# Up projection of a gated MLP with tokens on the output partitions, and each section's down projection one block later

## The chip, the cores and the metric

The kernel runs on one core of one Trainium2 chip. The metric is device time in microseconds (us), the median of several executions of the same program. Beside it there is one profiled execution, from which every row below is taken; its engines are PE (TensorE), DVE (VectorE), ACT (ScalarE), POOL (GpSimd) and SP (SyncE).

## The reference, cut to what matters

One decoder layer on 256 tokens of width 2048: a forgetting-attention mixer, then a gated MLP. Only the MLP and the step ahead of it change.

```python
h = h + fox_mixer(rms_norm(h, mix_norm), ...)          # q, k, v, attention, w_out
h = h + conv_ffn(rms_norm(h, ffn_norm), ...)

def conv_ffn(h, w_up, conv_w, conv_b, w_down):
    up = h @ w_up                                       # 256 x 2048 @ 2048 x 11264
    padded = jnp.pad(up, ((0, 0), (2, 0), (0, 0)))
    y = conv_b + conv_w[0] * padded[:, 0:seq]           # three causal taps along the tokens
    for tap in range(1, 3):
        y = y + conv_w[tap] * padded[:, tap:tap + seq]
    gate, val = jnp.split(y, 2, axis=-1)                # 5632 each
    return (jax.nn.silu(gate) * val) @ w_down           # 5632 x 2048
```

All of it is float32. The kernel multiplies with float32r operands: it splits every operand in a rounded part (hi) and the rest (lo) and adds three products, hi·hi, hi·lo and lo·hi.

## The kernel before, in words

**Weights.** `split_load` (L157) brings 1 MB (four k-rows of 128 by 512 columns) into one of four `raw` buffers through SP's DMA queue. ACT rounds it into `hi` and DVE subtracts to get `lo`, in two pieces of 128x1024 (two k-rows) each. There are five `hi` and five `lo` buffers (`HBUF`), so at most ten of a product's sixteen k-rows are prepared ahead of PE.

**Order.** The program is written as straight code. Work that is spread behind PE sits in the list `bg`, of which `tick` takes one step after every half of a weight load. The compiler's scheduler then orders each engine's instructions; each engine runs its own list in order.

**Output projection** (`out_part`, `out_evac`). Four column chunks c of 512; tokens are on the output partitions, with `mm_t` (L285): for each of the two token tiles t, three matmuls of 512 columns (L289 to L291), activations stationary and weights moving. `out_evac` adds the chunk to the residual `res`; the MLP wants it turned, channels on the partitions (`hs`). Chunks 0 to 2 are turned by DVE's transposes (32x32 squares in place, L315) and `spread` (L255), 16 DMAs from POOL that carry each 32x32 square to its place; chunk 3 is turned by PE (`h_turn`).

**Up projection** (`up_half`, `mm_run`). 11 blocks b of 512 gate columns ("ug") and 512 value columns ("uv"), a half being one of the two. Channels come out on the partitions: for each of the 16 k-rows and each 128 channels i, one matmul with `hi` stationary and both activation parts moving (512 columns, L278), and one with `lo` stationary and the rounded activations moving (256 columns, L280). `taps` adds the two parts (ACT copy L663, DVE add L664), multiplies by 1/rms of each token (`rhB`, L667, made by four PE matmuls in `spread_rstd`, L643), and does the three taps (ACT L669, DVE L673 twice). Then SiLU on ACT, the product, and the hi/lo split of the result `gt`.

**Down projection** (`down`). The 11 blocks form sections of 3, 3, 3 and 2. After the last block of a section its down projection runs with `mm_t`: four chunks of 512 output columns, over the section's 12 (or 8) k-rows.

Of the kernel before, what the change touches and what calls it, by code (L numbers as in the profile page):

```python
# [24 lines left out]
FT = FF // P  # L25
# [6 lines left out]
SECTIONS = [12, 12, 12, 8]  # L32
# [62 lines left out]
def trunk_kernel(  # L95
# [61 lines left out]
    def split_load(src, kk, n, name):  # L157
        raw = wraw.tile([P, WEL], F32, tag="raw", name=f"raw_{name}")
        nc.sync.dma_start(raw[:, 0 : kk * n], src)
        hv, lv = [], []  # L160
        step = max(1, HEL // n)
        for j in range(0, kk, step):
            w = min(step, kk - j)
            hi = whi.tile([P, HEL], F32R, tag="hi", name=f"hi_{name}_{j}")
            lo = wlo.tile([P, HEL], F32R, tag="lo", name=f"lo_{name}_{j}")
            src = raw[:, j * n : (j + w) * n]
            nc.scalar.copy(hi[:, 0 : w * n], src)  # L167
            nc.vector.tensor_tensor(  # L168
                lo[:, 0 : w * n], src, hi[:, 0 : w * n].bitcast(F32), op=ALU.subtract
            )  # L170
# [101 lines left out]
    hs = []  # L272
    hs_new = lambda: [acts.tile([P, 2, S], F32R, tag=f"as{k}", name=f"hs{k}") for k in range(KT)]


    def mm_run(run):
        for o, hv, lv, a, first, last in run:
            nc.tensor.matmul(o[:, 0:512], lhsT=hv, rhs=a.rearrange("p a s -> p (a s)"), start=first, stop=False)  # L278
        for o, hv, lv, a, first, last in run:
            nc.tensor.matmul(o[:, 0:S], lhsT=lv, rhs=a[:, 0, :], start=False, stop=last)  # L280

    wo = Blocks(w_out, blocks_out())


# [18 lines left out]
    def out_evac(pts, c):  # L303
        for t in range(NT):
            hc = res[:, t, c * 512 : (c + 1) * 512]
            nc.vector.tensor_tensor(hc, hc, pts[t], op=ALU.add)
            sq = hp_.tile([P, 512], F32, tag="hsq", name=f"hsq{c}_{t}")
            square(sq, t, c)
        if c == 3:
            bg.extend([nop, lambda: [h_turn(kp) for kp in (6, 7)]])  # L310
            return
        hq = tp.tile([P, 4 * NT, P], F32, tag="hq", name=f"hq{c}")
        hT = tp.tile([P, NT, 4, P], F32, tag="hT", name=f"hT{c}")
        for t in range(NT):
            nc.vector.transpose(  # L315
                hq[:, 4 * t : 4 * t + 4, :].rearrange("p k s -> p (k s)"), res[:, t, c * 512 : (c + 1) * 512]
            )
        spread(hT.rearrange("p t k s -> p (t k) s"), hq, nc.gpsimd)

        def scale():  # L320
            for j in range(4):
                k = 4 * c + j
                g, d = gffn[:, k : k + 1], hs[k].rearrange("p a (t s) -> p a t s", t=NT)
                nc.scalar.activation(d[:, 0], hT[:, :, j, :], AF.Copy, scale=g)
                nc.vector.scalar_tensor_tensor(
                    d[:, 1], hT[:, :, j, :], g, d[:, 0].bitcast(F32), op0=ALU.mult, op1=ALU.subtract,
                )
# [307 lines left out]
    nc.gpsimd.dma_start(convp.rearrange("p j f -> p (j f)"), conv)  # L635

    rh = const.tile([P, NT], F32, name="rh")
    rhB = const.tile([P, S], F32, name="rhB")

    def spread_rstd():  # L640
        prb = bank("prb")
        for t in range(NT):
            nc.tensor.matmul(  # L643
                prb[:, t * P : (t + 1) * P], lhsT=rh[:, t : t + 1].to_broadcast([P, P]), rhs=ident,
                start=True, stop=True,
            )
        nc.vector.tensor_copy(rhB, prb[:, 0:S])

    rms(rh)
    bg.extend([nop, spread_rstd])  # L650

    NPAD = 6
    pads = [fp.tile([P, S + 2], F32, name=f"pad{j}") for j in range(NPAD)]
    for j in range(NPAD):
        nc.gpsimd.memset(pads[j][:, 0:2], 0.0)
    npad = [0]

    wu = Blocks(w_up, blocks_up())
    wd = Blocks(w_down, blocks_down())

    def taps(pt, f, name):
        t = fp.tile([P, S], F32, tag="ut", name=f"ut{name}", bufs=2)
        nc.scalar.copy(t, pt[:, S:512])  # L663
        nc.vector.tensor_tensor(t, pt[:, 0:S], t, op=ALU.add)  # L664
        pad = pads[npad[0] % NPAD]
        npad[0] += 1
        nc.vector.tensor_tensor(pad[:, 2 : S + 2], t, rhB, op=ALU.mult)  # L667
        y = fp.tile([P, S], F32, tag="y", name=f"y{name}", bufs=4)
        nc.scalar.activation(  # L669
            y, pad[:, 0:S], AF.Identity, bias=convp[:, 3, f : f + 1], scale=convp[:, 0, f : f + 1]  # L670
        )
        for j in (1, 2):
            nc.vector.scalar_tensor_tensor(  # L673
                y, pad[:, j : j + S], convp[:, j, f : f + 1], y, op0=ALU.mult, op1=ALU.add
            )
        return y

    def gtile(b):
        return acts.tile([P, 2, 2, S], F32R, tag=f"os{b % 8}", name=f"gt{b}")

    def up_half(b, half, name):
        pts = [bank(f"p{name}{b}_{i}", ("mm", "sm")[i // 2]) for i in range(4)]
        for kb in range(4):
            hv, lv = split_load(wu[b, half, 4 * kb], 4, 512, f"{name}{b}_{kb}")
            mm_run([
                (pts[i], hv[j][:, i * P : (i + 1) * P], lv[j][:, i * P : (i + 1) * P],
                 hs[k], k == 0, k == KT - 1)
                for j, k in enumerate(range(kb * 4, kb * 4 + 4)) for i in range(4)
            ])
            tick()  # L690
            tick()
        return pts

    def up_block(b):
        sgs = []
        for i, pt in enumerate(up_half(b, 0, "ug")):
            f = 4 * b + i
            yg = taps(pt, f, f"g{f}")
            sg = fp.tile([P, S], F32, tag="sg", name=f"sg{f}", bufs=5)
            nc.scalar.activation(sg, yg, AF.Silu)  # L700
            sgs.append(sg)
        gts = []
        for i, pt in enumerate(up_half(b, 1, "uv")):
            f = 4 * b + i
            if i % 2 == 0:
                gpair = gtile(f // 2)
            yv = taps(pt, FT + f, f"v{f}")
            nc.vector.tensor_tensor(yv, sgs[i], yv, op=ALU.mult)
            gt = gpair[:, i % 2]
            nc.scalar.copy(gt[:, 0, :], yv)  # L710
            nc.vector.tensor_tensor(gt[:, 1, :], yv, gt[:, 0, :].bitcast(F32), op=ALU.subtract)
            gts.append(gt)
        return gts

    outv = out.rearrange("o (t p) d -> p (o t) d", p=P)

    def down(s, f0, gts, last):
        nk = len(gts)
        for c in range(4):
            pts = [bank(f"pd{s}_{c}_{t}", ("mm", "sm")[t]) for t in range(NT)]  # L720
            k0 = 0
            while k0 < nk:
                kk = min(4, nk - k0)
                hv, lv = split_load(wd[c, f0 + k0], kk, 512, f"d{s}_{c}_{k0}")
                for j in range(kk):
                    mm_t(pts, gts[k0 + j], hv[j], lv[j], k0 + j == 0, k0 + j == nk - 1)
                k0 += kk
            for t in range(NT):
                hc = res[:, t, c * 512 : (c + 1) * 512]
                nc.vector.tensor_tensor(hc, hc, pts[t], op=ALU.add)  # L730
                if last:
                    nc.sync.dma_start(outv[:, t, c * 512 : (c + 1) * 512], hc)

    f0 = 0
    for s, n in enumerate(SECTIONS):
        gts = []
        for b in range(n // 4):
            gts += up_block(f0 // 4 + b)
        while bg:
            tick()  # L740
        down(s, f0, gts, s == 3)
        f0 += n


# [47 lines left out]
```

## Time and profile before

| | us |
|---|---|
| device time, median of 3 runs | 1122.23 (1120.85 to 1123.55) |
| device time of the profiled execution | 1121.05 |
| its span, first to last instruction | 1119.3 |
| PE busy in the span | 1110.5 |
| DVE busy | 753.2 |
| ACT busy | 570.5 |
| POOL busy | 87.6 |

The profiled execution is 1.18 us below the median of the runs. "Busy" counts an engine's instructions only, not its waits; a matmul's end is modelled, so times of matmuls are best read from start to start.

### The profile page before, as it was taken

The page shows a single profiled execution, that of the slowest core. Times are in us where ns is not written, and L with a number is a line of the kernel's source. Part 1 is how long each engine was busy: PE and PEld are TensorE (multiplying, and loading weights), DVE is VectorE, ACT ScalarE, POOL GpSimd, SP SyncE. Part 2 cuts the span into 40 slices and gives each one's busy share as a digit, 9 for nine tenths or more (in the row PEclk, how much of TensorE's full clock was granted, in tenths as well). Part 3 has the DMA queues.
Part 4 walks back from the last instruction along what each step waited for, and adds up shares of the span by engine and source line. Part 5 has one row for each costly group of instructions (what it writes and reads, how often), then busy time and mean ns, then how long its engine had stood idle before and what let it go on. Part 6 is the DMA issues. An engine that isn't in the chain of part 4 may idle for free.

```text
span 1119.3 us, 15032 instructions
## 1 busy us (share of the span) xinstructions
PE 1110.5 (99%) x5672; PEld 950.0 (85%) x5672; DVE 753.2 (67%) x1210; ACT 570.5 (51%) x837; POOL 87.6 (8%) x152
## 2 busy tenths in 40 slices
PE   8999999999999999999999999999999999999998
PEld 6898888888888888888888888888888888888886
DVE  6666948677647658687655767765577777557864
ACT  7644545454535656565444555543455554346542
POOL 1102403030106400000000000000000000000000
PEclk9999999999999999999999999999999999999999
DMA  9839577677648645555555555555555555555542
GB/s 336 312 76 357 140 264 224 176 266 209 217 157 239 215 168 188 189 188 190 197 200 171 196 192 192 193 201 188 188 188 188 189 188 193 197 183 183 198 176 75
DMA packets 89145, 223.51 MB, mean 200 GB/s; under 512 B 58624, under 2 KB 58912, under 8 KB 64752
## 3 DMA queue, kind: packets, MB, share of 16 engines
q1 hardware_dynamic: 86640, 218.52, 57.8%
q0 software_dynamic: 2288, 4.01, 1.5%
q8 instruction: 44, 0.72, 0.2%
q14 instruction: 29, 0.24, 0.1%
q10 hardware_dynamic: 144, 0.02, 0.0%
HBM read 212.28 MB, written 2.11 MB: 192 GB/s over the span
## 4 chain that ended last, share of the span: by engine, by line
PE 96%; SPq 1%; DMA 1%; DVE 1%; ACT 0%; issue 0%; DVEq 0%
PE pug L278 14%; PE puv L278 14%; PE puv L280 8%; PE pug L280 7%; PE pd L290 7%; PE pd L289 7%; PE pd L291 7%; PE po L291 3%; PE pk L355 3%; PE pk L354 3%; PE po L290 3%; PE po L289 3%; PE pk L353 3%; PE pq L354 2%; PE pq L355 2%; PE pq L353 2%
## 5 line engine op out<-in xcount | busy, mean ns | idle before, releaser
L278 PE MATMUL puv<-hs,hi_uv 128*128 128x512 f32 x704 | 168.8, 391 | 1.2 <-ACT hi_uv L167 1.1
L278 PE MATMUL pug<-hs,hi_ug 128*128 128x512 f32 x704 | 167.9, 391 | 0.0
L168 DVE TENSOR_TENSOR lo_ug<-raw_ug,hi_ug 128x1024 fp32r<-128x1024 f32 x88 | 106.1, 1221 | 81.1 <-PE puv L280 36.8
L168 DVE TENSOR_TENSOR lo_d<-raw_d,hi_d 128x1024 fp32r<-128x1024 f32 x88 | 106.6, 1223 | 78.6 <-ACT hi_d L167 56.1
L278 PEld LDWEIGHTS puv<-hs,hi_uv 128*128 128x128 f32 x704 | 129.2, 188 | 26.9 <-ACT hi_uv L167 1.6
L278 PEld LDWEIGHTS pug<-hs,hi_ug 128*128 128x128 f32 x704 | 129.6, 188 | 25.2
L167 ACT CAST hi_d<-raw_d 128x1024 fp32r<-128x1024 f32 x88 | 92.2, 1052 | 114.8 <-PE pd L291 83.0
L167 ACT CAST hi_uv<-raw_uv 128x1024 fp32r<-128x1024 f32 x88 | 92.4, 1051 | 106.7 <-PE pug L278 63.2
L167 ACT CAST hi_ug<-raw_ug 128x1024 fp32r<-128x1024 f32 x88 | 92.6, 1052 | 105.9 <-PE puv L278 34.4
L168 DVE TENSOR_TENSOR lo_uv<-raw_uv,hi_uv 128x1024 fp32r<-128x1024 f32 x88 | 106.2, 1221 | 58.5 <-PE pug L280 47.2
L290 PE MATMUL pd<-lo_d,gt 128*128 128x512 f32 x352 | 136.2, 389 | 0.0
L289 PE MATMUL pd<-hi_d,gt 128*128 128x512 f32 x352 | 134.5, 389 | 0.0
L291 PE MATMUL pd<-hi_d,gt 128*128 128x512 f32 x352 | 134.2, 389 | 0.0
L280 PEld LDWEIGHTS puv<-hs,lo_uv 128*128 128x128 f32 x704 | 90.3, 191 | 3.4
L280 PEld LDWEIGHTS pug<-hs,lo_ug 128*128 128x128 f32 x704 | 90.3, 191 | 3.4
L280 PE MATMUL puv<-hs,lo_uv 128*128 128x256 f32 x704 | 91.5, 283 | 0.0
L280 PE MATMUL pug<-hs,lo_ug 128*128 128x256 f32 x704 | 91.3, 283 | 0.0
L291 PEld LDWEIGHTS pd<-hi_d,gt 128*128 128x128 f32 x352 | 66.1, 188 | 13.7
L289 PEld LDWEIGHTS pd<-hi_d,gt 128*128 128x128 f32 x352 | 66.1, 188 | 13.6
L290 PEld LDWEIGHTS pd<-lo_d,gt 128*128 128x128 f32 x352 | 66.1, 188 | 13.6
L168 DVE TENSOR_TENSOR lo_o<-raw_o,hi_o 128x1024 fp32r<-128x1024 f32 x32 | 39.1, 1222 | 34.2 <-ACT hi_o L167 33.8
L168 DVE TENSOR_TENSOR lo_q<-raw_q,hi_q 128x1024 fp32r<-128x1024 f32 (+1 forms) x33 | 38.8, 1187 | 27.0 <-ACT hi_q L167 27.0
(171 smaller groups left out, 1816.7 us busy)
## 6 DMA issues: line engine op xcount, KB each, us to landing
raw_ug<-in_w_up SPq DMA_DIRECT2D x44, 1024.0 KB, 4.9
raw_uv<-in_w_up SPq DMA_DIRECT2D x44, 1024.0 KB, 4.9
raw_d<-in_w_down SPq DMA_DIRECT2D x44, 1024.0 KB, 4.8
raw_k<-in_w_in SPq DMA_DIRECT2D x16, 1024.0 KB, 8.8
raw_o<-in_w_out SPq DMA_DIRECT2D x16, 1024.0 KB, 5.6
raw_q<-in_w_in SPq DMA_DIRECT2D x12, 1024.0 KB, 6.0
raw_v<-in_w_in SPq DMA_DIRECT2D x12, 1024.0 KB, 5.7
raw_q<-in_w_in SPq DMA_DIRECT2D x7, 512.0 KB, 6.8
```

What stands on the lines that cost most here:

```text
L167: nc.scalar.copy(hi[:, 0 : w * n], src)
L168: nc.vector.tensor_tensor(lo[:, 0 : w * n], src, hi[:, 0 : w * n].bitcast(F32), op=ALU.subtract)
L278: nc.tensor.matmul(o[:, 0:512], lhsT=hv, rhs=a.rearrange("p a s -> p (a s)"), start=first, stop=False)
L280: nc.tensor.matmul(o[:, 0:S], lhsT=lv, rhs=a[:, 0, :], start=False, stop=last)
L289: nc.tensor.matmul(pts[t], lhsT=ah, rhs=hv, start=first, stop=False)
L290: nc.tensor.matmul(pts[t], lhsT=ah, rhs=lv, start=False, stop=False)
L291: nc.tensor.matmul(pts[t], lhsT=al, rhs=hv, start=False, stop=last)
L353: nc.tensor.matmul(o, lhsT=ah, rhs=hv[j], start=(k == 0), stop=False)
L354: nc.tensor.matmul(o, lhsT=ah, rhs=lv[j], start=False, stop=False)
L355: nc.tensor.matmul(o, lhsT=al, rhs=hv[j], start=False, stop=(k == KT - 1))
```

## The change

The up projection takes the form of the output projection: tokens on the output partitions, `hs` stationary, weights moving, three matmuls of 512 columns a token tile (`mm_t`), two PSUM banks a half where there were four. 1/rms of a token is now a per-partition scale of the evacuation (ACT), so `rhB`, its matmuls and the multiply go. The half is then turned: two DVE transposes of 128x512, and `spread` from POOL. `taps` reads the turned tile, without a pad. The taps of a half (`gates`, `values`) are written behind the matmuls of the next half or of the next weight load in `down`. Down projections of sections 0 and 1 are written behind the first block of the next section. Chunk 2 of the output projection is turned by PE like chunk 3.

```diff
-        if c == 3:
-            bg.extend([nop, lambda: [h_turn(kp) for kp in (6, 7)]])
+        if c >= 2:
+            bg.extend([nop, lambda: [h_turn(kp) for kp in (2 * c, 2 * c + 1)]])
             return
...
     def up_half(b, half, name):
-        pts = [bank(f"p{name}{b}_{i}", ("mm", "sm")[i // 2]) for i in range(4)]
+        pts = [bank(f"p{name}{b}_{t}", "mm") for t in range(NT)]
         for kb in range(4):
             hv, lv = split_load(wu[b, half, 4 * kb], 4, 512, f"{name}{b}_{kb}")
-            mm_run([
...
+            for j in range(4):
+                k = 4 * kb + j
+                mm_t(pts, hs[k], hv[j], lv[j], k == 0, k == KT - 1)
             tick()
             tick()
+        uq = tp.tile([P, 4, NT, P], F32, tag="hq", name=f"q{name}{b}")
+        uT = tp.tile([P, 4, S], F32, tag="hT", name=f"T{name}{b}")
+        for t in range(NT):
+            nc.scalar.activation(
+                uq[:, :, t, :], pts[t].rearrange("p (f d) -> p f d", d=P), AF.Copy, scale=rh[:, t : t + 1]
+            )
+        for f in range(0, 4, 2):
+            q = uq[:, f : f + 2].rearrange("p f t d -> p (f t d)")
+            nc.vector.transpose(q, q)
+        spread(
+            uT.rearrange("p f (t s) -> p (f t) s", t=NT), uq.rearrange("p f t d -> p (f t) d"), nc.gpsimd
+        )
+        return uT
...
+    def taps(u, f, name):
+        y = fp.tile([P, S], F32, tag="y", name=f"y{name}", bufs=4)
+        nc.scalar.activation(y, u, AF.Identity, bias=convp[:, 3, f : f + 1], scale=convp[:, 2, f : f + 1])
+        for j in (1, 0):
+            d = 2 - j
+            nc.vector.scalar_tensor_tensor(
+                y[:, d:S], u[:, 0 : S - d], convp[:, j, f : f + 1], y[:, d:S], op0=ALU.mult, op1=ALU.add
+            )
+        return y
...
+    def up_block(b):
+        for half, name, use in ((0, "ug", gates), (1, "uv", values)):
+            uT = up_half(b, half, name)
+            product_done()
+            later.append(lambda uT=uT, use=use: use(b, uT))
...
+                if k0 == 0:
+                    product_done()
...
+    behind = [ends[0] + 1, ends[1] + 1, FT // 4, FT // 4]
+    done = 0
     for s, n in enumerate(SECTIONS):
-        gts = []
-        for b in range(n // 4):
-            gts += up_block(f0 // 4 + b)
...
+        while done < behind[s]:
+            up_block(done)
+            done += 1
+        down(s, starts[s], n, s == len(SECTIONS) - 1)
```

How this changes the engines' lists is shown at three places, all in the second block or at its edge. Numbers behind a name are buffer numbers; a name's own indices stand before them (`hi_ug_1_0` is weight load 1, k-row 0 of that load).

PE, the start of the second block's gate half, before: of a weight load's 32 rows, the first of 512 and the first of 256 columns.

```order
L278 MATMUL pug_0_4009<-hs_2726,hi_ug_0_0_4015 128x512
L278 MATMUL pug_1_4010<-hs_2726,hi_ug_0_0_4015 128x512
L278 MATMUL pug_2_4011<-hs_2726,hi_ug_0_0_4015 128x512
L278 MATMUL pug_3_4012<-hs_2726,hi_ug_0_0_4015 128x512
L278 MATMUL pug_0_4009<-hs_2727,hi_ug_0_0_4015 128x512
...
L278 MATMUL pug_3_4012<-hs_2729,hi_ug_0_2_4019 128x512
L280 MATMUL pug_0_4009<-hs_2726,lo_ug_0_0_4016 128x256
```

The same place in the changed kernel: of a weight load's 24 rows, those of the first k-row.

```order
L282 MATMUL pug_0_3896<-hi_ug_0_0_3900,hs_2726 128x512
L283 MATMUL pug_0_3896<-lo_ug_0_0_3901,hs_2726 128x512
L284 MATMUL pug_0_3896<-hi_ug_0_0_3900,hs_2726 128x512
L282 MATMUL pug_1_3897<-hi_ug_0_0_3900,hs_2726 128x512
L283 MATMUL pug_1_3897<-lo_ug_0_0_3901,hs_2726 128x512
L284 MATMUL pug_1_3897<-hi_ug_0_0_3900,hs_2726 128x512
```

Per half PE issues 96 matmuls of 512 columns where it issued 64 of 512 and 64 of 256; the lo weights are wanted one matmul after the hi weights, where they were wanted 16 matmuls after.

ACT, behind the second block's gate half, before: PSUM copies (`utg`), taps (`yg`), SiLU (`sg`) and rounding of weights (`hi`) alternate.

```order
L663 COPY utg_4181<-pug_0_4009 128x256
L663 COPY utg_4191<-pug_1_4010 128x256
L167 CAST hi_uv_2_2_4315<-raw_uv_2_4309 128x1024
L669 ACTIVATE yg_4185<-pad_3547,convp 128x256
L663 COPY utg_4201<-pug_2_4011 128x256
L669 ACTIVATE yg_4195<-pad_3548,convp 128x256
L663 COPY utg_4211<-pug_3_4012 128x256
L167 CAST hi_uv_3_0_4353<-raw_uv_3_4351 128x1024
```

ACT in the changed kernel, where the second block's value half (`puv`) ends and the third block's gate half is being prepared; `Tug` is the second block's turned gate half.

```order
L167 CAST hi_ug_1_2_4312<-raw_ug_1_4306 128x1024
L649 ACTIVATE quv_4224<-puv_0_4086,rh 128x4x128
L662 ACTIVATE yg_4246<-Tug_4035,convp 128x256
L662 ACTIVATE yg_4252<-Tug_4035,convp 128x256
L662 ACTIVATE yg_4258<-Tug_4035,convp 128x256
L662 ACTIVATE yg_4264<-Tug_4035,convp 128x256
L649 ACTIVATE quv_4224<-puv_1_4087,rh 128x4x128
L167 CAST hi_ug_2_0_4342<-raw_ug_2_4340 128x1024
```

The taps of a gate half now stand one half later, between the two evacuations of the value half, and the rounding of the next half's fifth weight piece (`hi_ug_2_0`) stands behind all of them.

DVE at that same edge in the changed kernel.

```order
L168 TENSOR_TENSOR lo_ug_1_2_4313<-raw_ug_1_4306,hi_ug_1_2_4312 128x1024
L665 SCALAR_TENSOR_TENSOR yg_4246<-Tug_4035,convp,yg_4246 128x255
L665 SCALAR_TENSOR_TENSOR yg_4252<-Tug_4035,convp,yg_4252 128x255
...
L665 SCALAR_TENSOR_TENSOR yg_4258<-Tug_4035,convp,yg_4258 128x254
L654 STREAM_TRANSPOSE quv_4224<-quv_4224 128x512 x2
L665 SCALAR_TENSOR_TENSOR yg_4264<-Tug_4035,convp,yg_4264 128x254
L168 TENSOR_TENSOR lo_ug_2_0_4343<-raw_ug_2_4340,hi_ug_2_0_4342 128x1024
```

Seven of the gate half's eight taps, the two transposes of the value half and the eighth tap stand ahead of `lo_ug_2_0`, which before was made ahead of any of them.

## Rows read from the trace of the kernel before

**Rows 1.** The page's first lines and its chain that ended last.

```profile
span 1119.3 us, 15032 instructions
PE 1110.5 (99%) x5672; PEld 950.0 (85%) x5672; DVE 753.2 (67%) x1210; ACT 570.5 (51%) x837; POOL 87.6 (8%) x152
PE 96%; SPq 1%; DMA 1%; DVE 1%; ACT 0%; issue 0%; DVEq 0%
```

**Rows 2.** The chain in order of time, section 1: start us, us, what.

```profile
584.90 3.63 PE pug L278 x16
588.52 1.91 PE pug L280 x16
590.44 3.65 PE pug L278 x16
...
716.56 1.91 PE puv L280 x16
718.47 0.23 PE pd L289
...
783.78 3.63 PE pug L278 x16
```

**Rows 3.** Windows: us, busy of PE, PEld, DVE, ACT, POOL, clock, DMA share, GB/s.

```profile
584.90:718.47 133.57, 133.57 (x769) 118.06 (x769) 91.73 (x146) 73.49 (x111) 0.00 (x0) 1.00 0.55 189
718.47:783.78 65.31, 65.31 (x289) 54.08 (x289) 41.94 (x56) 28.25 (x35) 0.00 (x0) 1.00 0.56 194
```

**Rows 4.** The chain where the first block starts: start us, us, what.

```profile
388.46 0.87 PE ht L228 x8
```

**Rows 5.** PE's timeline a little later: start us, us, line and what, idle before.

```profile
395.67 0.61 PE L643 MATMUL prb<-ident,rh 128*128 128x128 f32 x4
396.04 1.50 PE L278 MATMUL puv<-hs,hi_uv 128*128 128x512 f32 x4
398.67 2.11 PE L278 MATMUL puv<-hs,hi_uv 128*128 128x512 f32 x8 [1.14 <-ACT hi_uv L167]
```

**Rows 6.** Groups of ACT: operation, form, count | busy us, mean ns | idle before.

```profile
L167 ACT CAST hi_ug<-raw_ug 128x1024 fp32r<-128x1024 f32 x88 | 92.6, 1052 | 105.9 <-PE puv L278 34.4 <-PE pug L278 33.8 <-PE pd L291 25.0
L669 ACT ACTIVATE yg<-pad,convp 128x256 f32<-128x256 f32 x44 | 26.3, 598 | 0.0
L663 ACT COPY utg<-pug 128x256 f32<-128x256 f32 x44 | 14.9, 365 | 5.3 <-PE pug L280 5.3
L406 ACT ACTIVATE ksb<-pk,rx 128x512 f32<-128x512 f32 x8 | 5.4, 686 | 3.1 <-PE pk L355 2.2 <-DMA T<-qsb 1.0
```

**Rows 7.** Groups of DVE, in the same columns.

```profile
L168 DVE TENSOR_TENSOR lo_ug<-raw_ug,hi_ug 128x1024 fp32r<-128x1024 f32 x88 | 106.1, 1221 | 81.1 <-PE puv L280 36.8 <-ACT hi_ug L167 24.8 <-PE pug L280 19.6
L673 DVE SCALAR_TENSOR_TENSOR yg<-pad,convp,yg 128x256 f32<-128x256 f32 x88 | 41.2, 478 | 7.1 <-ACT yg L669 7.1
L711 DVE TENSOR_TENSOR gt<-yv,gt 128x256 fp32r<-128x256 f32 x44 | 18.4, 419 | 1.4 <-ACT gt L710 0.5
L667 DVE TENSOR_TENSOR pad<-utg,rhB 128x256 f32<-128x256 f32 x44 | 17.4, 417 | 0.0
L664 DVE TENSOR_TENSOR utg<-pug,utg 128x256 f32<-128x256 f32 x44 | 17.4, 416 | 0.0
L315 DVE STREAM_TRANSPOSE hq<-res 128x512 f32<-128x512 f32 x6 | 4.0, 689 | 0.0
```

**Rows 8.** The tile hT, target of three spreads: duration ns min/median/max, waits, landing.

```profile
L258 POOL DMA_DIRECT2D hT<-hq x48: 582/582/622, 342.2 to 376.3; - x48
...
  DMA hT<-hq: 6.1, 6
...
DMA to landing us min/median/max: 1.9/4.4/7.4
```

**Rows 9.** Windows around those three spreads, columns as in rows 3.

```profile
354.00:377.00 23.00, 23.00 (x103) 19.07 (x102) 14.79 (x17) 11.25 (x17) 17.79 (x31) 1.00 0.90 255
342.00:377.00 35.00, 35.00 (x156) 29.01 (x155) 22.47 (x25) 17.21 (x24) 27.63 (x48) 1.00 0.87 249
```

**Rows 10.** DMA issues: what, from which queue, count, KB each, us to landing.

```profile
raw_ug<-in_w_up SPq DMA_DIRECT2D x44, 1024.0 KB, 4.9
raw_o<-in_w_out SPq DMA_DIRECT2D x16, 1024.0 KB, 5.6
```

More of the change, by code (lines that the diff above doesn't have):

```diff
@@ L273, in trunk_kernel @@
     hs_new = lambda: [acts.tile([P, 2, S], F32R, tag=f"as{k}", name=f"hs{k}") for k in range(KT)]
[L276 to L280, printed above, removed]
     wo = Blocks(w_out, blocks_out())
@@ L327, in scale @@
                 )
-        bg.extend([nop] * (4, 3, 6)[c] + [scale])
+        bg.extend([nop] * (4, 3)[c] + [scale])
     with tc.tile_pool(name="att", bufs=2) as att, tc.tile_pool(name="ckp", bufs=1) as ckp:
@@ L637, in trunk_kernel @@
     rh = const.tile([P, NT], F32, name="rh")
[L638 to L647, printed above, removed]
-    rms(rh)
-    bg.extend([nop, spread_rstd])
-    NPAD = 6
-    pads = [fp.tile([P, S + 2], F32, name=f"pad{j}") for j in range(NPAD)]
@@ L654, in trunk_kernel, with up_half @@
-    for j in range(NPAD):
-        nc.gpsimd.memset(pads[j][:, 0:2], 0.0)
-    npad = [0]
+    rms(rh)
     wu = Blocks(w_up, blocks_up())
     wd = Blocks(w_down, blocks_down())
[L661 to L667, printed above, removed]
+    def up_half(b, half, name):
+        pts = [bank(f"p{name}{b}_{t}", "mm") for t in range(NT)]
+        for kb in range(4):
+            hv, lv = split_load(wu[b, half, 4 * kb], 4, 512, f"{name}{b}_{kb}")
+            for j in range(4):
+                k = 4 * kb + j
+                mm_t(pts, hs[k], hv[j], lv[j], k == 0, k == KT - 1)
+            tick()
+            tick()
+        uq = tp.tile([P, 4, NT, P], F32, tag="hq", name=f"q{name}{b}")
[11 more added lines that the diff above has]
+        return uT
@@ L668, in taps @@
+    def taps(u, f, name):
         y = fp.tile([P, S], F32, tag="y", name=f"y{name}", bufs=4)
[L669 to L672, printed above, removed]
+        nc.scalar.activation(y, u, AF.Identity, bias=convp[:, 3, f : f + 1], scale=convp[:, 2, f : f + 1])
+        for j in (1, 0):
+            d = 2 - j
             nc.vector.scalar_tensor_tensor(
-                y, pad[:, j : j + S], convp[:, j, f : f + 1], y, op0=ALU.mult, op1=ALU.add
+                y[:, d:S], u[:, 0 : S - d], convp[:, j, f : f + 1], y[:, d:S], op0=ALU.mult, op1=ALU.add
@@ L675, in taps @@
             )
         return y
-    def gtile(b):
-        return acts.tile([P, 2, 2, S], F32R, tag=f"os{b % 8}", name=f"gt{b}")
-    def up_half(b, half, name):
-        pts = [bank(f"p{name}{b}_{i}", ("mm", "sm")[i // 2]) for i in range(4)]
-        for kb in range(4):
-            hv, lv = split_load(wu[b, half, 4 * kb], 4, 512, f"{name}{b}_{kb}")
-            mm_run([
[L686 to L692, printed above, removed]
@@ L694, in up_block, with gates @@
-    def up_block(b):
-        sgs = []
-        for i, pt in enumerate(up_half(b, 0, "ug")):
-            f = 4 * b + i
[L698 to L701, printed above, removed]
-        gts = []
-        for i, pt in enumerate(up_half(b, 1, "uv")):
+    gts = {}
+    sgs = {}
+    def gates(b, uT):
+        for i in range(4):
+            f = 4 * b + i
+            yg = taps(uT[:, i, :], f, f"g{f}")
+            sgs[f] = fp.tile([P, S], F32, tag="sg", name=f"sg{f}", bufs=6)
+            nc.scalar.activation(sgs[f], yg, AF.Silu)
@@ L704, in up_block, with values @@
+    def values(b, uT):
+        for i in range(4):
             f = 4 * b + i
             if i % 2 == 0:
[L706 to L709, printed above, removed]
+                n = (f // 2) % 10
+                pool = acts if n < 8 else fp
+                gpair = pool.tile([P, 2, 2, S], F32R, tag=f"os{n}", name=f"gt{f // 2}")
+            yv = taps(uT[:, i, :], FT + f, f"v{f}")
+            nc.vector.tensor_tensor(yv, sgs[f], yv, op=ALU.mult)
+            gts[f] = gt = gpair[:, i % 2]
@@ L710, in up_block @@
             nc.scalar.copy(gt[:, 0, :], yv)
             nc.vector.tensor_tensor(gt[:, 1, :], yv, gt[:, 0, :].bitcast(F32), op=ALU.subtract)
-            gts.append(gt)
-        return gts
     outv = out.rearrange("o (t p) d -> p (o t) d", p=P)
-    def down(s, f0, gts, last):
-        nk = len(gts)
-        for c in range(4):
[L720 to L727, printed above, removed]
+    later = deque()
@@ new lines, in product_done, with down @@
+    def product_done():
+        while later:
+            later.popleft()()
+    def up_block(b):
[3 more added lines that the diff above has]
+            later.append(lambda uT=uT, use=use: use(b, uT))
+    def down(s, f0, nk, last):
+        for c in range(4):
+            pts = [bank(f"pd{s}_{c}_{t}") for t in range(NT)]
+            for k0 in range(0, nk, 4):
+                hv, lv = split_load(wd[c, f0 + k0], 4, 512, f"d{s}_{c}_{k0}")
+                for j in range(4):
+                    mm_t(pts, gts[f0 + k0 + j], hv[j], lv[j], k0 + j == 0, k0 + j == nk - 1)
+                if k0 == 0:
+                    product_done()
@@ L732, in down @@
                     nc.sync.dma_start(outv[:, t, c * 512 : (c + 1) * 512], hc)
-    f0 = 0
+    starts = [sum(SECTIONS[:s]) for s in range(len(SECTIONS))]
+    ends = [sum(SECTIONS[: s + 1]) // 4 for s in range(len(SECTIONS))]
+    behind = [ends[0] + 1, ends[1] + 1, FT // 4, FT // 4]
+    done = 0
     for s, n in enumerate(SECTIONS):
-        gts = []
-        for b in range(n // 4):
-            gts += up_block(f0 // 4 + b)
[L739 to L742, printed above, removed]
+        while done < behind[s]:
+            up_block(done)
+            done += 1
+        down(s, starts[s], n, s == len(SECTIONS) - 1)
 def kernel(**inputs):
```

## Prediction

> **What bounds the kernel now.** The page first: PE is busy 1110.5 of 1119.3 us, and the chain that ended last is 96% PE [rows 1]. So only PE's own work and its waits count; other engines matter where they make PE wait. Next the chain in order of time, for what PE does in a block: runs of 16 matmuls of 512 columns (3.65 us, 228.1 ns each) and runs of 16 of 256 columns (1.91 us, 119.4 ns each), end on end [rows 2]. Halving the columns does not halve the time: 256 columns more cost 108.7 ns, so some 10.7 ns of each matmul is not columns. Last the windows of a section's up and down projection: PE is busy all of 133.57 and all of 65.31 us, at a granted clock of 1.00 (the higher of two levels, 2.4 GHz) [rows 3]. There is no stall in them that could be removed. The clock is no term: what follows keeps PE as dense as before.
>
> **The change, part by part.**
>
> *Matmuls of the up projection.* Columns do not change: a half had 64 x 512 + 64 x 256 = 49,152, and has 96 x 512 = 49,152. Their number falls from 128 to 96. Before, three blocks are six halves, from 584.90 to 718.47: 22.26 us a half [rows 2, 3]. For the new form the trace has a row: the down projection runs the same `mm_t`, 4 x 12 x 6 = 288 matmuls from 718.47 to 783.78, 226.8 ns each [rows 2, 3]. 96 of them are 21.77 us. A half saves 0.49 us, 22 halves 10.8 us. The other bound is the price of the up projection's own wide matmuls, 228.1 ns: 21.90 us a half, 8.0 us in all. I take 10.8, since `pd` is the same code with the same operand roles. The Trainium skill differs here (TensorE: Matmul & The Clock Gate, "Wait — 56ns, not 53.3ns?"): a fixed cost of about 2.5 ns a matmul, so that 22 x 32 = 704 fewer would give 1.8 us. By the rows it would be some 10 ns, and I go by the rows.
>
> *Around the start of the up projection.* The four `spread_rstd` matmuls go: 395.67 to 396.04, 0.4 us of PE [rows 5]. Turning chunk 2 on PE adds eight transposes; the eight of chunk 3 took 0.87 us [rows 4]. They stand four k-rows (5.4 us) into chunk 3, and need only chunk 2's two adds, so no wait. Sum: 0.5 us more. In exchange chunk 2's two DVE transposes, its 16 POOL transfers and the wait for them go. PE's only wait at this place, 1.14 us ahead of 398.67 on `hi_uv` [rows 5], comes from a list in which value matmuls had been moved ahead of the gate half's end. In the new list the gate half runs through; its last k-rows (12 on) come 16 us after its start, and need two adds, eight transposes and ACT and DVE's halves, some 9 us. I take the 1.14 as gained; the bounds are 0 and 1.14.
>
> *Evacuation and taps.* ACT loses eight copies of 0.365 us a block and gets four evacuations of 128x512 from PSUM with a scale; the nearest is `ksb`, 0.69 us [rows 6]: 2.9 out, 2.8 in. DVE loses eight adds and eight multiplies (0.417 each, 6.7 us) and gets four transposes of 0.69 (2.8 us) [rows 7]. Its sum a block was 16 x 1.221 + 16 x 0.478 + 16 x 0.417 + 8 x 0.419 = 37.2 us of 44.5; now 33.3 of 43.5. All of it lies beside PE, so it is worth nothing by itself.
>
> *The transfers.* 352 DMAs of 32 KB go onto POOL's queue; nothing else stands there in this stage, and SP's list is only reordered by section. The same transfers ran in the output projection: 0.58 us to issue, 1.9 to 7.4 us to land, median 4.4 [rows 8], while PE stayed busy for all of 35.00 us [rows 9]. Three spreads raised the DMA share there from 0.55 [rows 3] to 0.87 over 35 us, 3.7 us of all queues each; one a half makes 0.55 + 3.7/21.8 = 0.72. A weight load landed in 5.6 us there against 4.9 [rows 10], with four buffers of 5.4 us each ahead. Hidden.
>
> *What now waits for the transfer.* Let a gate half end at T. ACT evacuates until T + 1.4, DVE has turned it at T + 2.8. POOL issues eight, then each waits for the one eight places earlier (the waits of 6.1 us on the same transfer [rows 8]). With a landing of L over 4.6 us the last of 16 lands at 2.8 + 7 x 0.58 + 2L = 6.9 + 2L: T + 21.7 at the longest L seen, 7.4. ACT wants the turned tile at T + 21.8 + 0.7 = T + 22.5, between the evacuations of the value half. So even the longest landing costs nothing. Behind those taps stands the rounding of the next half's fifth piece. Count from that half's start U = T + 21.8: four taps at 0.60 until 3.1, evacuation 3.8, `hi` 4.8; DVE's seven taps until 4.7, transposes 6.0, eighth tap 6.5, `lo` 7.7 [rows 6, 7]. PE wants it at k-row 8, 8 x 6 x 0.2268 = 10.9. The slack is 3.2 us, the smallest I find; behind the gate half it is over 5 us. If the cover were gone, every block would pay the excess.
>
> *Down one block later.* The rows before show no wait at the section's edge, so nothing is gained there. It is needed: the last values of a section are ready some 30 us after their matmuls (evacuation, turn, transfer, taps), and without the move PE would wait about that at each edge. Behind the next block (43.5 us), or at the end behind section 2's down projection (65.3), it costs 0.
>
> **Sum.** 1119.3 - 10.8 - 1.1 + 0.5 = 1107.9 us of span. The profiled execution took 1.75 us more than its span: 1109.6. The median of the runs lay 1.18 above it: **1110.8 us**. Its own range is 1109 to 1114, from the two rates of a matmul, the wait at the start and the spread of the runs.
>
> **Rivals.**
>
> *The turned tile comes late (slower).* Place: ACT's first `yg` of a half, with the weight rounding queued behind it. With landing L, PE waits once 6.9 + 2L is over 22.5 + 3.2, L = 9.4 us, and pays the excess in each of 11 blocks. At L = 9.9 it has eaten the gain of 1.0 us a block; at 12 us it is 5.2 x 11 = 57 us, about 1168. For it: all 352 transfers now run beside weight loads, in pieces of 128 bytes. Against: in a window with a DMA share of 0.90 [rows 9] the longest of 48 took 7.4 [rows 8], and here the share is lower. The Trainium skill (DMA: Bandwidth & Descriptors, opening table) wants at least 512 bytes a piece for line rate; the raised share in rows 9 agrees, and is priced above.
>
> *DVE comes late with lo (a smaller gain).* The lo piece is wanted one matmul after hi, where a run of 16 (3.65 us) lay between [rows 2]. If a value half's chain (eight taps, eight products and subtractions, 7.2 us) overlaps badly with the eight lo pieces, PE waits some 0.4 us a block: 4.4 us, 1115. Against: DVE's sum falls, and the down projection with the same demand has no idle PE [rows 3].
>
> *Fewer matmuls save nothing.* If PE's time went by columns alone, the half would stay at 22.26 and only 1.1 - 0.5 = 0.6 us be gained: 1121.6, the same. Against: 119.4 is far over half of 228.1 [rows 2]. By the 2.5 ns of the page cited above, it would be 1.8 us less than that, 1119.8.
>
> **How the numbers follow.** The forecast has 0.83, late lo 0.08, late transfers 0.05, nothing saved 0.04. A difference within 0.2% (2.2 us) cannot be told from none. The forecast and late lo are faster, and part of the third case's mild form: 0.92. Nothing saved and the edge of late transfers are the same: 0.04. Slower is late transfers: 0.04. The range takes the forecast's bounds and late lo: 1108.5 to 1115.
>
> **What the changed profile would show.** Right: 96 matmuls a half at 226.8 ns, 21.8 us from half to half, windows of the up projection with PE busy throughout; POOL's `Tug` and `Tuv` landing under 8 us; no wait of `yg` on a transfer that reaches PE; DMA share near 0.72; the chain still 96% PE. Wrong: PE idle ahead of a matmul on `hi_ug_2_0` or `lo_ug_2_0`, released in the end by a DMA into `Tug`; matmuls of 228 ns or more; or a wait of `pd` on `gt` at a section's edge.

## The result and the profile after

The changed kernel takes 1109.53 us (median of four runs, 1109.08 to 1111.77); the kernel before, run beside it, 1121.73 (four runs, 1120.85 to 1123.55). The ratio is 0.9895, its 95% interval 0.9879 to 0.9911: faster by 1.05%. The forecast was 1110.8.

The profiled execution took 1109.87 us. Its page begins:

```profile
span 1108.2 us, 13923 instructions
PE 1100.4 (99%) x4972; PEld 913.5 (82%) x4972; DVE 724.2 (65%) x1075; ACT 571.8 (52%) x793; POOL 281.0 (25%) x482
...
PE 97%; SPq 1%; DMA 1%; DVE 0%; ACT 0%; issue 0%
```

Against [rows 1] PE has 700 matmuls fewer (704 of the up projection and four of `spread_rstd`, less eight more of the turn) and is busy 10.1 us less, and the span is 11.1 us shorter. PE still ends the chain. POOL is busy 281.0 us where it was 87.6, DVE 29 us less.

Where a product's name changes in PE's timeline, a half or a down projection begins (start us, us, line and what): the first block's value half, the second block's gate half, and both ends of the down projections of sections 0 and 1.

```profile
406.31 0.39 PE L282 MATMUL puv<-hi_uv,hs 128*128 128x512 f32 x1
...
428.07 0.39 PE L282 MATMUL pug<-hi_ug,hs 128*128 128x512 f32 x1
...
558.63 0.39 PE L282 MATMUL pd<-hi_d,gt 128*128 128x512 f32 x1
...
623.91 0.39 PE L282 MATMUL pug<-hi_ug,hs 128*128 128x512 f32 x1
...
754.47 0.39 PE L282 MATMUL pd<-hi_d,gt 128*128 128x512 f32 x1
...
820.42 0.39 PE L282 MATMUL pug<-hi_ug,hs 128*128 128x512 f32 x1
```

From 406.31 to 428.07 a half takes 21.76 us; the six halves from 428.07 to 558.63 take 130.56, 21.76 each. Before, it was 22.26 [rows 2, 3]. The windows, in the columns of [rows 3], show that PE has no hole there:

```profile
406.45:428.00 21.55, 21.55 (x97) 17.85 (x96) 10.99 (x10) 9.48 (x11) 9.26 (x16) 1.00 0.73 220
...
428.07:558.63 130.56, 130.56 (x577) 108.11 (x576) 92.02 (x132) 78.25 (x110) 55.37 (x96) 1.00 0.71 218
558.63:623.91 65.28, 65.28 (x289) 54.05 (x288) 42.93 (x57) 32.26 (x42) 9.23 (x16) 1.00 0.61 202
754.47:820.42 65.95, 65.95 (x289) 54.15 (x288) 42.92 (x57) 32.22 (x42) 9.22 (x16) 1.00 0.60 200
```

The DMA share rose to 0.71 to 0.73, from 0.55. The whole list of PE's waits (engine, what, released by whom: us in total, times, longest) no longer has the wait on `hi_uv` of [rows 5], nor any other in the MLP:

```profile
PE pq L346 <- ACT hi_q L167: 1.6, 2, 1.0
PE pw L212 <- DVE zeros L209: 1.3, 1, 1.3
PE pq L347 <- DVE lo_q L168: 0.5, 1, 0.5
PE po L506 <- issue: 0.2, 1, 0.2
```

The new operations, in the columns of [rows 6] and [rows 7], and the landing of the transfers into the two turned tiles (us, min/median/max; first `Tug`, then `Tuv`), to be read beside [rows 8]:

```profile
L649 ACT ACTIVATE qug<-pug,rh 128x512 f32<-128x512 f32 x22 | 15.0, 690 | 10.9 <-PE pug L284 10.9
L654 DVE STREAM_TRANSPOSE qug<-qug 128x512 f32<-128x512 f32 x22 | 14.4, 691 | 12.4 <-ACT qug L649 12.4
```

```profile
DMA to landing us min/median/max: 1.9/4.6/6.4
...
DMA to landing us min/median/max: 1.8/5.3/8.7
```

Last the place at which a late tile would show. ACT and then DVE around the end of the third block's value half (which ends at 515.11; the order is that of the second block's), timeline:

```profile
514.63 0.69 ACT L649 ACTIVATE quv<-puv,rh 128x512 f32<-128x512 f32 x1 [0.94 <-PE puv L284]
515.22 2.07 ACT L662 ACTIVATE yg<-Tug,convp 128x256 f32<-128x256 f32 x4
517.19 0.67 ACT L649 ACTIVATE quv<-puv,rh 128x512 f32<-128x512 f32 x1
517.76 1.04 ACT L167 CAST hi_ug<-raw_ug 128x1024 fp32r<-128x1024 f32 x1
```

```profile
515.84 2.95 DVE L665 SCALAR_TENSOR_TENSOR yg<-Tug,convp,yg 128x255 f32<-128x255 f32 x7 [0.89 <-ACT yg L662]
518.71 1.30 DVE L654 STREAM_TRANSPOSE quv<-quv 128x512 f32<-128x512 f32 x2
519.93 0.44 DVE L665 SCALAR_TENSOR_TENSOR yg<-Tug,convp,yg 128x254 f32<-128x254 f32 x1
520.29 3.49 DVE L168 TENSOR_TENSOR lo_ug<-raw_ug,hi_ug 128x1024 fp32r<-128x1024 f32 x3
```

`yg` starts without a wait on the transfer, and ACT's list of waits has no `yg` or `yv` on a transfer anywhere. The first of the three `lo` pieces at 520.29 is that of `lo_ug_2_0`, ready some 1.2 us later, at 521.5. PE wants it at the ninth k-row, 515.11 + 8 x 6 x 0.2267 = 526.0: 4.5 us to spare. Of the 264 `lo` pieces of the MLP none comes closer to the matmul that reads it.

### The profile page after: what moved, and what is told of

Its sections match the earlier page's. It is cut to its first block, busy times and chain, and to the rows that moved or that the text cites. A ratio compares the mean times of both kernels' runs of the same rounds, so it can differ in the third digit from the quotient of the medians.

```text
span 1108.2 us, 13923 instructions
## 1 busy us (share of the span) xinstructions
PE 1100.4 (99%) x4972; PEld 913.5 (82%) x4972; DVE 724.2 (65%) x1075; ACT 571.8 (52%) x793; POOL 281.0 (25%) x482
## 4 chain that ended last, share of the span: by engine, by line
PE 97%; SPq 1%; DMA 1%; DVE 0%; ACT 0%; issue 0%
PE pd L284 7%; PE pd L283 7%; PE puv L283 7%; PE pd L282 7%; PE pug L283 7%; PE pug L284 7%; PE puv L284 7%; PE pug L282 7%; PE puv L282 7%; PE po L282 3%; PE pk L347 3%; PE po L284 3%; PE pk L348 3%; PE po L283 3%; PE pk L346 3%; PE pq L347 2%
## 5 line engine op out<-in xcount | busy, mean ns | idle before, releaser
L258 POOL DMA_DIRECT2D Tug<-qug x176 | 101.6, 584 | 256.7 <-ACT hi_uv L167 216.6
L258 POOL DMA_DIRECT2D Tuv<-quv x176 | 101.5, 584 | 164.8 <-ACT sg L678 143.9
L284 PE MATMUL pd<-hi_d,gt 128*128 128x512 f32 x352 | 137.4, 390 | 0.0
L282 PE MATMUL pd<-hi_d,gt 128*128 128x512 f32 x352 | 137.4, 390 | 0.0
L282 PE MATMUL pug<-hi_ug,hs 128*128 128x512 f32 x352 | 137.0, 389 | 0.0
L284 PE MATMUL pug<-hi_ug,hs 128*128 128x512 f32 x352 | 137.0, 389 | 0.0
L282 PE MATMUL puv<-hi_uv,hs 128*128 128x512 f32 x352 | 136.9, 389 | 0.0
L283 PE MATMUL puv<-lo_uv,hs 128*128 128x512 f32 x352 | 136.9, 389 | 0.0
L284 PE MATMUL puv<-hi_uv,hs 128*128 128x512 f32 x352 | 136.9, 389 | 0.0
L283 PE MATMUL pug<-lo_ug,hs 128*128 128x512 f32 x352 | 136.9, 389 | 0.0
L282 PEld LDWEIGHTS puv<-hi_uv,hs 128*128 128x128 f32 x352 | 66.1, 188 | 13.8
L282 PEld LDWEIGHTS pug<-hi_ug,hs 128*128 128x128 f32 x352 | 66.1, 188 | 13.7
```

The lines of the kernel that those rows point to most:

```text
L258: q.dma_start(dst[d * SQ : (d + 1) * SQ, :, o * SQ : (o + 1) * SQ], src[o * SQ : (o + 1) * SQ, :, d * SQ : (d + 1) * SQ],)
L282: nc.tensor.matmul(pts[t], lhsT=ah, rhs=hv, start=first, stop=False)
L283: nc.tensor.matmul(pts[t], lhsT=ah, rhs=lv, start=False, stop=False)
L284: nc.tensor.matmul(pts[t], lhsT=al, rhs=hv, start=False, stop=last)
```

## Experiments

Single runs stand beside a run of the kernel before on the same chip; their difference to the changed kernel is told from the span of the profiled execution (1108.2) too.

### Is it the number of matmuls?

`e1_same_count` takes the changed kernel and cuts one of the three matmuls of a token tile, the one with `lo`, into two of 256 columns. A half has the 64 wide and 64 narrow matmuls that it had before, in the new form.

```diff
+    def mm_up(pts, a, hv, lv, first, last):
...
+            nc.tensor.matmul(pts[t], lhsT=ah, rhs=hv, start=first, stop=False)
+            for o in (0, 256):
+                nc.tensor.matmul(
+                    pts[t][:, o : o + 256], lhsT=ah, rhs=lv[:, o : o + 256], start=False, stop=False
+                )
+            nc.tensor.matmul(pts[t], lhsT=al, rhs=hv, start=False, stop=last)
...
-                mm_t(pts, hs[k], hv[j], lv[j], k == 0, k == KT - 1)
+                mm_up(pts, hs[k], hv[j], lv[j], k == 0, k == KT - 1)
```

> The changed kernel, but in the up projection each matmul of the rounded activations with the lo weights is cut in two of 256 columns: a half has 64 matmuls of 512 and 64 of 256 columns again, as many as the kernel before, in the new form (tokens on the output partitions). Theory, the gain is the number of matmuls: 64 x 0.2268 + 64 x 0.1194 = 22.16 us a half against 21.77, so 8.5 us more, about 1118 us. Rival, the gain comes from the form and not from the number (columns alone count): 1109.5 us, as the changed kernel. Second rival, a fixed cost of 2.5 ns a matmul: 704 x 2.5 ns = 1.8 us more, 1111.3.

Measured: 1122.04 us (ten runs), the kernel before 1121.43 (thirteen); the ratio to before is 1.0002 (0.9993 to 1.0012). The whole gain is gone, with the new layout, transposes and transfers all in place. PE's chain in that run (start us, us, what; the pair of narrow ones is one entry):

```profile
451.98 0.23 PE puv L641
452.22 0.23 PE puv L643 x2
452.44 0.23 PE puv L646
452.68 0.23 PE puv L641
```

A token tile takes 0.70 us (452.68 - 451.98) where three wide matmuls take 0.68, and PE waits for nothing in the stretch. The span is 11.5 us longer than that of the changed kernel, over 704 added matmuls 16 ns each. This is more than the 8.5 us that I had expected. The pair of narrow ones is not dearer than I had put it: it takes 0.23 us, 115 ns each. The wide ones beside them are dearer, 0.233 us each (start to start, mean of three blocks) where they take 0.227 among themselves; before the change, too, the wide ones took more in the mix, 228.1 ns [rows 2].

`e2_all_halved` cuts nearly all of them (188 narrow and 2 wide a half).

```diff
...
+                for o in (0, 256):
+                    nc.tensor.matmul(
+                        pts[t][:, o : o + 256], lhsT=l, rhs=r[:, o : o + 256],
+                        start=False, stop=e and o == 256,
+                    )
...
```

> The changed kernel with every matmul of the up projection but the first two of a half cut in two of 256 columns: 188 of 256 and 2 of 512 a half. Theory (a matmul of 256 columns takes 119.4 ns): 22.90 us a half, 1.13 us more, 24.9 us in all, 1134. Columns alone: 1109.5. Fixed cost of 2.5 ns a matmul: 94 x 22 x 2.5 ns = 5.2 us, 1114.7.

Measured: 1137.61 us, span 1135.9, 27.7 more than the changed kernel for 22 x 94 = 2068 more matmuls: 13.4 ns each. PE's chain:

```profile
454.37 5.75 PE puv L646 x48
```

That is 119.8 ns a narrow matmul; two of them take 12.9 ns more than a wide one of 226.7. The number of matmuls (each with the load of its own stationary operand, which these two runs add with it) is the cause of the gain, not the form of the product. Which share is the load's and which the matmul's, no run tells.

### What the start of the up projection gives

`e6_turn2_only` is the kernel before with chunk 2 turned by PE; `e8_chunk2_dve` is the changed kernel with chunk 2 turned by DVE and transfers, as before.

```diff
-        if c >= 2:
-            bg.extend([nop, lambda: [h_turn(kp) for kp in (2 * c, 2 * c + 1)]])
+        if c == 3:
+            bg.extend([nop, lambda: [h_turn(kp) for kp in (6, 7)]])
...
-        bg.extend([nop] * (4, 3)[c] + [scale])
+        bg.extend([nop] * (4, 3, 6)[c] + [scale])
```

> The kernel before with one part of the change alone: chunk 2 of the output projection is turned by PE. Theory: the wait of 1.14 us at the start of the up projection goes and eight transposes of 0.87 us come: 0.3 us less, not to be told by time; the trace shows PE without a wait between 380 and 410 us. Rival: the wait comes from the order of PE's list there and stays; then PE has both.

> The changed kernel with chunk 2 of the output projection turned by DVE and transfers again. Theory: PE loses eight transposes, 0.9 us less; its k-rows 8 to 11 are wanted 11 us into the first half, when the transfers have landed, so no wait in the trace; 1108.6, within what time can tell. Rival: the late rows make PE wait again, some 1 us or more.

Measured: `e6_turn2_only` 1122.39 us (before 1123.07), and the wait of 1.14 us is not among PE's waits; the time is not told apart from no change in one run. `e8_chunk2_dve` 1113.64 us, span 1111.9. That is not what I had expected of it: in its timeline the wait stands at the old place.

```profile
396.23 0.39 PE L284 MATMUL pug<-hi_ug,hs 128*128 128x512 f32 x1
397.79 0.73 PE L282 MATMUL puv<-hi_uv,hs 128*128 128x512 f32 x2 [1.18 <-ACT hi_uv L167]
399.05 0.50 PE L283 MATMUL puv<-lo_uv,hs 128*128 128x512 f32 x1 [0.53 <-DVE lo_uv L168]
399.39 0.40 PE L284 MATMUL puv<-hi_uv,hs 128*128 128x512 f32 x1
```

So the wait belongs to chunk 2's turn by transfers, after which value matmuls are put ahead of the gate half's end, and not to `spread_rstd` or to the old product. Of the 3.7 us of span that this run lost, 1.9 are a longer wait in the attention stage (2.1 us on `pT` where the changed kernel had 0.2), which the edit does not touch. Start to start the four matmuls from 396.23 to 399.39 took 3.16 us instead of 0.91, so PE lost 2.25 us here, more than the 1.7 that the list of waits has; less the 0.87 of eight transposes that went, this place cost 1.4.

### The turn on PE instead

`e7_turn_on_pe` turns each half with eight PE transposes and two ACT copies, with no transfers.

```diff
-        for f in range(0, 4, 2):
-            q = uq[:, f : f + 2].rearrange("p f t d -> p (f t d)")
-            nc.vector.transpose(q, q)
-        spread(
...
+                        nc.tensor.transpose(
+                            pt[:, j * S + t * P : j * S + (t + 1) * P], uq[:, f + j, t, :], ident
+                        )
+                nc.scalar.copy(uT[:, f : f + 2, :].rearrange("p f s -> p (f s)"), pt)
```

> The changed kernel with each half turned by eight PE transposes (behind the next half's first weight load) and two ACT copies from PSUM, without DVE's transposes and the transfers. Theory, PE is the bound and whatever it gets is paid: 22 x 0.87 = 19.1 us more, about 1129, slower than the kernel before. Rival, the transfers had cost PE something that now comes back: under 1120.

Measured: 1131.14 us (before 1123.07), PE busy 20.1 us more than in the changed kernel, 0.91 us a half where I had 0.87. With the turn on PE in this way the change is slower than the kernel before: the new product pays only because the turn lies beside PE.

### How late the turned tile may come

Two kernels keep POOL busy ahead of a gate half's transfers with copies of one column onto itself, 22 and 65 of them.

```diff
+        if half == 0:
+            for _ in range(22):
+                nc.gpsimd.tensor_copy(uq[:, 0, 0, 0:1], uq[:, 0, 0, 0:1])
```

> The changed kernel with 22 copies of one column in place on POOL between the gate half's transposes and its spread; at 184 ns each the transfers start 4 us later in gate halves. Theory, slack of some 6.5 us: no change, 1109.5, though ACT now waits for the transfer. Rival, PE waits as soon as ACT waits (22.6 us after the half): 1.3 us a block, 14 us, about 1124.

> The changed kernel with 65 copies of one column in place on POOL between the gate half's transposes and its spread; at 184 ns each the transfers start 12 us later in gate halves. Theory, slack of some 6.5 us from the last landing (20 us after the half) to the moment from which PE waits (26.4 us): 5.5 us a block, 60 us in all, about 1170, with PE idle ahead of hi_ug_2_0 or lo_ug_2_0. Rival, no slack behind ACT's reading at 22.6 us: 9.3 us a block, 102 us. Second rival, hidden anyway: 1109.5.

Measured: 1110.49 us (before 1123.07) and 1122.51. Neither was the delay that I had meant. A copy took 0.42 to 0.51 us in its chain, so that POOL was held for some 9 and some 27 to 30 us; and the compiler put copies and transfers in another order and moved the readers of the tile back. With 22 copies POOL's timeline shows

```profile
504.65 9.18 POOL L657 COPY qug<-qug 128x1 f32<-128x1 f32 x18
514.19 0.58 POOL L258 DMA_DIRECT2D Tug<-qug  x1 [0.35 <-POOL qug L657]
516.00 1.73 POOL L258 DMA_DIRECT2D Tug<-qug  x3 [1.23 <-issue]
```

where the changed kernel issued its last three from 506.28. ACT's first `yg` came at 522.30, 28.8 us behind the start of the gate half's evacuation (493.53); in the changed kernel it is 22.4 (492.87 to 515.22). ACT's list has the rounding of `hi_ug_2_0` and of the piece behind it ahead of that `yg` now, so this run does not show how much delay the old list would have borne. PE waited for nothing in the MLP. With 65 copies ACT waited for the tiles, and PE in the end for `lo` pieces (lists of waits of PE and of ACT):

```profile
PE puv L283 <- DVE lo_uv L168: 4.3, 4, 1.7
PE pd L283 <- DVE lo_d L168: 3.1, 2, 1.6
...
ACT yg L665 <- DMA Tuv<-quv: 52.3, 7, 8.4
ACT yg L665 <- DMA Tug<-qug: 29.3, 4, 8.3
```

The chain of the rival is there: tile late, taps late, rounding queued behind them, `lo` late, PE idle for 7.4 us in all. Its price is far below the 60 or 102 us that I had expected. The span is 12.6 us longer; PE's busy time is 4.8 us longer too. In the 4.5 us behind the first of these waits, the longest, the granted clock was 0.62; behind the other five, of 0.4 to 1.6 us, it was 1.00.

```profile
510.50:515.00 4.50, 4.48 (x13) 3.53 (x14) 4.50 (x4) 2.93 (x4) 4.50 (x8) 0.62 0.90 278
```

### How much DVE may do

`e9_turn_x3` and `e10_turn_x7` let DVE turn each half three and seven times (an odd number of turns gives the same tile).

```diff
-            nc.vector.transpose(q, q)
+            for _ in range(3):
+                nc.vector.transpose(q, q)
```

> The changed kernel, in which DVE turns every half three times instead of once (turning the squares twice more gives the same tile): four more transposes of 0.65 us a half, 5.2 us a block. Theory (DVE's work lies beside PE): DVE has some 33 of 43.5 us a block, with this 38.5, and the turned tile comes 2.6 us later, under the 3.8 us of slack: as the changed kernel, 1109.5 (to 1111). Rival (late lo: DVE's list at the edge of a half has no room): 1 us or more a block, over 1120.

> The changed kernel, in which DVE turns every half seven times instead of once: twelve more transposes of 0.65 us a half, 15.6 us a block. Theory: DVE has then some 49 of 43.5 us a block and is the bound in the blocks; 5.4 us x 11 = 59 us if nothing is caught up in the down projections, where DVE has 42 of 65 us, and little if all is: between 1120 and 1170, with PE waiting on lo pieces. Rival (only PE's matmuls count, whatever DVE does): 1109.5.

Measured: 1111.24 and 1111.38 us (before 1120.58), spans 1109.0 and 1109.6. The first is as the theory had it, with no wait of PE in the MLP. The second is not: I had set at least 1120. PE waits 0.8 us once in the MLP. Two halves (the second block's value half and the third's gate half) in the changed kernel, and then the same stretch and that of section 1's down projection in `e10_turn_x7`, where they begin 0.4 and 1.4 us later:

```profile
449.83:493.35 43.52, 43.52 (x193) 36.04 (x192) 30.61 (x44) 25.66 (x37) 18.45 (x32) 1.00 0.70 218
```

```profile
449.83:493.35 43.52, 43.52 (x194) 36.04 (x193) 42.43 (x66) 24.85 (x35) 13.31 (x24) 1.00 0.63 197
754.47:820.42 65.95, 65.95 (x290) 54.10 (x289) 54.88 (x84) 35.98 (x50) 18.46 (x32) 1.00 0.64 201
```

DVE is full in the two halves (42.43 of 43.52 us), and the down projection takes what is left over (54.88 us where the changed kernel has 42.92 there). In DVE's list the added transposes stand in ones, twos and threes between single `lo` pieces, so the pieces that PE wants next keep their turn.

### Down projections at their old places

`e3_old_edges` puts each section's down projection directly behind its own last block.

```diff
-    behind = [ends[0] + 1, ends[1] + 1, FT // 4, FT // 4]
+    behind = ends
```

> The changed kernel with each down projection right behind its own section's last block, as before the change. Theory: PE waits for the last block's gt; but the compiler's scheduler can put chunk 1's ready rows into the gap (2 x 10.9 us of ready work at three edges, 2 x 5.4 at the last), and the first gt comes some 23 us, the last 27 us after the value half: 3 x 3 + 14 = 23 us more, about 1132 (1125 to 1150). Rival, as the prediction had it: about 30 us at each of four edges, 120 us, 1230. Second rival, no loss: 1109.5.

Measured: 1148.23 us, span 1146.5, 38.3 more. PE waits for `gt` at each of the four edges, 26.1 us in all, the longest 10.7. The first edge in PE's timeline:

```profile
538.69 0.39 PE L284 MATMUL pd<-hi_d,gt 128*128 128x512 f32 x1
544.21 0.80 PE L282 MATMUL pd<-hi_d,gt 128*128 128x512 f32 x1 [5.14 <-ACT gt L690]
544.80 0.63 PE L283 MATMUL pd<-lo_d,gt 128*128 128x512 f32 x1
545.23 0.63 PE L282 MATMUL pd<-hi_d,gt 128*128 128x512 f32 x1
```

The compiler had filled 21.9 us (517.2 to 539.1) of the 30 with those k-rows of the down projection whose values were ready. The rest was a wait, and what followed it ran slowly (windows of that edge):

```profile
530.00:539.00 9.00, 9.00 (x41) 7.17 (x39) 4.22 (x4) 3.17 (x3) 2.30 (x4) 1.00 0.83 252
...
544.21:548.30 4.09, 4.09 (x11) 3.27 (x11) 3.04 (x9) 1.15 (x3) 0.00 (x0) 0.55 0.00 0
```

The granted clock is 0.55 there, near the lower level of 1.2 GHz, and a matmul takes 0.43 us (544.80 to 545.23) instead of 0.227. PE's busy time is 11.6 us longer in this run; with the 26.1 us of waits that is 37.7 of the 38.3. I had expected 23 us, all of it waiting; the slow matmuls behind the waits were not in that sum.

## Why the prediction was right

**Matmuls of the up projection.** The step held, and by its number: 21.76 us a half for the 21.77 taken from the down projection, 11.1 us in 22 halves for the 10.8 forecast. `e1_same_count` shows the cause. The rival that fewer matmuls save nothing falls with it. One reading beside it was too low: 10.7 ns of a matmul that are not columns would give 7.5 us for 704 matmuls. It was taken where wide and narrow ones are mixed; in uniform runs it is 12.9. 704 matmuls more cost 11.5 us and 2068 more 27.7. The Trainium skill (TensorE: Matmul & The Clock Gate, "Wait — 56ns, not 53.3ns?") has some 2.5 ns of fixed cost a matmul at the higher clock; this trace does not agree, and the measurement decides.

**The start.** The second block begins at 428.07; before it began at 430.36, from an output projection at the same place in both (329.7). Two halves are 1.0 us of these 2.3, so the start gave some 1.3 where the prediction had 0.6 (1.14 + 0.4 - 0.87, rounded). The term that was too small is the wait: the list of waits counts it from the modelled end of a matmul. Start to start, the twelve wide matmuls from 396.04 [rows 5] to the next row of that timeline of the kernel before,

```profile
400.62 1.11 PE L280 MATMUL puv<-hs,lo_uv 128*128 128x256 f32 x8
```

took 4.58 us, where twelve of 228.1 ns take 2.74. So 1.84 us were lost around the wait, and 1.84 + 0.37 - 0.87 is the 1.3. The wait is gone, and `e8_chunk2_dve` brings it back. I had left it to the new list as a whole; the run shows that the turn of chunk 2 decides it.

**Down projection.** I had given it no term, and it has one: section 1's takes 65.95 us for the same 288 matmuls that took 65.28 in section 0, at a granted clock of 1.00. The last two together are 0.6 us longer than before as well. The trace shows which matmuls pay. Section 1's down projection begins at 754.47; 24, 48 and 72 matmuls later PE's timeline has

```profile
759.92 0.40 PE L282 MATMUL pd<-hi_d,gt 128*128 128x512 f32 x1
...
765.51 0.39 PE L282 MATMUL pd<-hi_d,gt 128*128 128x512 f32 x1
...
770.96 0.39 PE L282 MATMUL pd<-hi_d,gt 128*128 128x512 f32 x1
```

The second 24 take 5.59 us, those on either side 5.45, and so in each of the four chunks. They are the k-rows 4 to 7, whose `gt`, the stationary operand, lies in two buffers that the change adds: it has ten pairs of `gt` where there were eight, and the two new ones come from another pool (`fp`). In section 3 it is the k-rows 0 to 3, in the same two buffers; sections 0 and 2 do not use them and take 65.28 and 65.29. 192 matmuls at some 6.5 ns are the whole 1.25 us, and the same k-rows are the slow ones in `e1_same_count`, `e4_delay_short` and `e9_turn_x3`. Why these buffers are slower stays open: no run places them elsewhere.

**The sum.** The span came out at 1108.2 for the 1107.9 forecast partly by luck: the matmuls gave 0.3 us more than their term and the start 0.7, the down projection took 1.25 that had none.

**Transfers.** Priced at a DMA share of 0.72, measured 0.70 to 0.73 in a block; median landings of 4.6 and 5.3 us against 4.4 before. The longest, 8.7 us, passed the 8 that I had named, on the value half's tile, and cost nothing: the last transfer of a half landed at least 2.4 us ahead of the tile's first reading. `yg` was forecast 22.5 us behind the gate half's end (493.35) and came 21.9 behind it, since ACT takes the half's first token tile while PE ends the second. The slack at `lo_ug_2_0`, forecast as the smallest at 3.2 us, is the smallest and measures 4.5. It is a limit only for the list as it stands: in `e4_delay_short` the tile was read 6.4 us later without a wait of PE, and in `e10_turn_x7` a full DVE did not reach PE. DVE is busy 30.6 us in a block, where I had summed 33.3: the 44 operations are all there, 33.2 us by their single times, but back to back each begins some 0.06 us before the one ahead has ended. The prices that I gave to the rivals of late tile and late `lo` took the lists as fixed, and were too high; that the mechanism exists shows in `e5_delay_long`.

**Down one block later.** Needed, as said: without it 38.3 us, more than the change gains. The prediction's 30 us of waiting at each edge was too much: it left out that ready k-rows fill most of it, and the waits were 5.1 us at three edges and 10.7 at the last.

**From span to median.** 1.18 us were added because the profiled execution of before lay below its median. After, it lay 0.34 above it. That was chance, 1.5 us of it, and more than the 1.3 us by which the forecast is off.

## What to carry to other kernels

Where PE has no holes, count its matmuls and not only their columns: the same 49,152 columns in 96 matmuls instead of 128 took 0.5 us less, and the row that prices the new form was in the trace already, in another stage of the same kernel. Work moved to idle engines and queues was free here up to a full DVE, as long as what PE needs next kept its place in the lists; read slack from the lists, but expect the compiler to weave a changed program anew. Price a wait from start to start, as the list of waits can have less than PE loses. When a result gets a longer way to its reader, the reader has to move behind other work too: the move of the down projection gained nothing and was worth 38 us.

## What the runs showed of the hardware

At a granted clock of 1.00 a matmul of 512 columns took 226.7 ns and one of 256 took 119.8, each among its like. The 256 columns between them are 106.9 ns, close to one column a cycle of 2.4 GHz (106.7); what is left of either matmul is some 13 ns. Among narrow ones the wide took 233 ns and the narrow 115 (`e1_same_count`). In the stretch at the lower clock of `e3_old_edges` seven matmuls of 512 columns went from 545.01 to 548.00 in the chain, 427 ns each, and 512 columns at 1.2 GHz are 426.7: nothing is left over. The Trainium skill (TensorE: Matmul & The Clock Gate, "Wait — 56ns, not 53.3ns?") says the same of the lower clock, start to start exactly the columns. There this trace agrees; on the size at the higher clock it does not.

A wait can cost PE more than its length. The granted clock was 0.55 in the 4.1 us behind one of 5.1 us, and 0.62 in the 4.5 us behind one of 1.7; behind five of 0.4 to 1.6 us in the same run it stayed 1.00. A one-column copy on POOL took 0.42 to 0.51 us when each had to follow the one before, where a single one had taken 0.18.

Two matmuls of one form need not cost the same: with the stationary operand in two buffers of `gt` 24 took 5.59 us, with it in the others 5.45.
